# One-input affine steps of a mixer: from VectorE to ScalarE, or folded into their neighbours

## The chip, the core and the metric

The kernel runs on one core of one Trainium2 chip. The metric is the device time of one execution in microseconds (us), the median of several runs. The core's engines are TensorE (PE, with PEld for its weight loads), VectorE (DVE), ScalarE (ACT), GpSimd (POOL) and SyncE (SP), which here issues the DMAs. Each engine works through its own instructions strictly in the order in which they stand; semaphores hold an instruction back until what it reads is there and what it overwrites has been read.

## What is computed

A decoder trunk of two layers over 256 positions of width 1024, in float32. Each layer is a mixer with three branches, a LayerNorm, a retrieval over 16384 one-neuron experts (PEER), and a second LayerNorm. The change lies in the mixer, in its branches A and B:

```python
p = x @ w_in[l]                                   # one input projection, split among the branches
# A: depthwise causal conv of width 4, gates r and i, a linear recurrence, gelu of a second projection
xc = causal_depthwise_conv(xb, conv_w, conv_b)
r = sigmoid(xc @ wa + ba);  i = sigmoid(xc @ wx + bx)
log_a = -8 * r * softplus(-log_a_param)
h = scan(exp(log_a), sqrt(-expm1(2 * log_a)) * (i * xc));   y_a = h * gelu(gb)
# B: RWKV-7, 8 heads of 64
w = -softplus(-(w0 + tanh(xw) @ w2)) - 0.5;  a = sigmoid(a0 + xa @ a2)
kk = k * k_k;  kk = kk / norm(kk, per head);  k = k * (1 + (a - 1) * k_a)
state = state * exp(-exp(w)) - (state @ kk) x (kk * a) + v x k;  y = state @ r
yn = (y - mean) * rsqrt(var + eps) * gn_g + gn_b
y_b = (yn + bonus) * g
# C: latent attention -> y_c;  then merged = sum of sigmoid(gate_n) * (y_n @ P_n), times w_out, LayerNorm
```

## The kernel before, in words

Channels lie on the 128 partitions and positions along the free axis, so a mixer tensor of 512 channels is a tile of 128 x 4 x 256. Every weight tile of 128x1024 comes by DMA into `raw` and is split into two float32r parts: ACT makes `hi` (L84, a cast) and DVE makes `lo = raw - hi` (L88; POOL does so in part of PEER). A projection (`projecting`, L247 to L249) is then 24 matmuls of 128x256, three for each eighth of the contraction: hi times x-high, hi times x-low, lo times x-high. The two PSUM buffers `mm` take the results, so a projection can only start when the one two places before it has been read.

The mixer (function `mixer`) mixes a long chain with many independent projections. The chain is branch B: `rwkv_prep` (decay, keys, gates; L463 to L593), then `rwkv_scan`, which works in four chunks of 64 positions. Before the chunks it inverts a triangular matrix for each head and half chunk by substitution: 31 steps of a multiply (L613) and an add (L615) on DVE, each of which reads the one before, and then transposes up to the tile `t1u` (L623), which TensorE needs for the next matmuls (L638). After the chunks the result `yt` is normalised per head: a Newton iteration for the inverse square root on 128x16 (L172 to L176), `head_bcast` (a copy that repeats each head's value over 64 columns, `hex`, L310, and four transposes on PE, L313), a multiply (L710), the affine step with gn_g and gn_b (L712), two tensor steps (L713, L714) and the split into `ybh` and `ybl` (tiles k and at), which `branch(1, ...)` multiplies with its weights. Everything else is filler: the generators `latent` (branch C), `rg_prep`, `rg_gate` and `rg_scan` (branch A; conv in L729 and L731, gates from L747, gelu from L789), `gates1` and `branch` for branches 2 and 0. `fill(n)` draws n steps from them at points of the chain.

The order that results on the engines is not the order of the source. The framework that builds the program places the instructions of each engine by a schedule of its own when the program is built; on the chip that order is fixed. So an edit of one line can move the instructions around it.

`rsqrt`, `split` and `stream` are shared helpers, so their lines (L84, L88, L166 to L176) stand for many uses; the tile names tell them apart (`wo` is a weight tile of branch 1 or of the output projection).

## Time and profile before

| | |
|---|---|
| median of 3 runs | 2335.33 us (2332.97 to 2336.89) |
| the profiled execution: its own time | 2339.72 us |
| its span, first to last instruction | 2338.0 us |
| PE busy | 2242.7 us, 96% of the span |
| DVE busy | 1790.2 us, 77% |
| ACT busy | 1088.5 us, 47% |
| POOL busy | 278.4 us, 12% |
| mean granted TensorE clock | 0.979 of full speed |

The mixer of layer 0 fills the span from its start to about 345 us, that of layer 1 from about 1170 to 1515 us; PEER lies between and behind. Matmuls overlap each other and their ends are modelled, so a busy PE is not a PE at its peak, but a gap in its row is real. In the clock column 1.00 is full speed (2.4 GHz) and 0.50 the lower level (1.2 GHz).

### The profile page before, as it was taken

The numbers are of one execution on the slowest core, as the hardware profiler recorded it, in microseconds if no ns is written. First come the engines' busy times: TensorE is split into PE (matmuls) and PEld (weight loads), VectorE is DVE, ScalarE is ACT, GpSimd is POOL, SyncE is SP. The second block draws the span as 40 slices with busy tenths as digits, with TensorE's granted clock in tenths as the row PEclk, the third lists the DMA queues.
The fourth block names the chain that finished last, engine by engine and source line by source line (L and its number), as shares of the span: only waits on it lengthen the run. The fifth ranks groups of instructions, "written<-read, shape, count | busy, mean of one in ns | idle before, by whom it ended". The sixth has DMA issues, their size and how long they took to land. (4 is left out here: it accounts for less than half of the span.)

```text
span 2338.0 us, 39856 instructions
## 1 busy us (share of the span) xinstructions
PE 2242.7 (96%) x15748; PEld 1980.1 (85%) x15748; DVE 1790.2 (77%) x3268; ACT 1088.5 (47%) x1635; POOL 278.4 (12%) x220
## 2 busy tenths in 40 slices
PE   7999989999999999999899999899999999999998
PEld 6888879998888888888787888799988888888886
DVE  6777877966788888755666877789668888887556
ACT  4543534445555544444445534344455555444443
POOL 0010016930000000000000100179300000000000
PEclk9998999999999999999999989999999999999999
DMA  6323344555555555655552234445555555556554
GB/s 212 118 79 113 133 164 146 165 184 185 175 170 172 173 176 170 213 196 190 189 174 91 91 109 134 160 142 170 183 184 177 172 171 172 174 171 214 194 193 136
DMA packets 104925, 381.88 MB, mean 163 GB/s; under 512 B 11649, under 2 KB 12161, under 8 KB 104481
## 3 DMA queue, kind: packets, MB, share of 16 engines
q1 hardware_dynamic: 104736, 379.32, 48.7%
q8 instruction: 124, 2.03, 0.3%
q14 instruction: 65, 0.52, 0.1%
HBM read 374.56 MB, written 4.72 MB: 162 GB/s over the span
## 5 line engine op out<-in xcount | busy, mean ns | idle before, releaser
L84 ACT CAST hi<-raw 128x1024 fp32r<-128x1024 f32 x658 | 690.3, 1050 | 756.2 <-PE acc L262 343.7
L88 DVE TENSOR_TENSOR lo<-raw,hi 128x1024 fp32r<-128x1024 f32 x570 | 696.0, 1222 | 250.0 <-ACT hi L84 242.5
L262 PE MATMUL acc<-hi,a 128*128 128x512 f32 x2000 | 554.6, 392 | 0.9 <-ACT a L166 0.9
L247 PE MATMUL mm<-xt,hi 128*128 128x256 f32 x1760 | 516.3, 294 | 23.7 <-ACT hi L84 11.7
L249 PE MATMUL mm<-xt,lo 128*128 128x256 f32 x1760 | 508.5, 290 | 13.9 <-DVE lo L88 10.5
L248 PE MATMUL mm<-xt,hi 128*128 128x256 f32 x1760 | 507.5, 288 | 0.0
L994 PE MATMUL acc<-xt,hi 128*128 128x512 f32 x1344 | 474.4, 399 | 0.0
L262 PEld LDWEIGHTS acc<-hi,a 128*128 128x128 f32 x2000 | 370.9, 188 | 76.2 <-ACT a L166 1.2
L247 PEld LDWEIGHTS mm<-xt,hi 128*128 128x128 f32 x1760 | 345.3, 196 | 31.0 <-ACT hi L84 11.7
L249 PEld LDWEIGHTS mm<-xt,lo 128*128 128x128 f32 x1760 | 344.3, 196 | 20.1 <-DVE lo L88 12.5
L997 PE MATMUL acc<-xt,lo 128*128 128x256 f32 x1344 | 348.7, 280 | 0.0
L248 PEld LDWEIGHTS mm<-xt,hi 128*128 128x128 f32 x1760 | 345.4, 196 | 2.1 <-issue 0.8
L262 PE MATMUL acc<-lo,a 128*128 128x512 f32 x1000 | 311.4, 391 | 0.0
L994 PEld LDWEIGHTS acc<-xt,hi 128*128 128x128 f32 x1344 | 245.4, 188 | 44.4
L88 POOL TENSOR_TENSOR lo<-raw,hi 128x512 fp32r<-128x512 f32 x176 | 251.5, 1455 | 244.9 <-ACT hi L84 243.2
L997 PEld LDWEIGHTS acc<-xt,lo 128*128 128x128 f32 x1344 | 253.5, 189 | 12.1
L262 PEld LDWEIGHTS acc<-lo,a 128*128 128x128 f32 x1000 | 187.7, 188 | 40.6 <-DVE lo L88 0.2
L1002 ACT COPY H<-acc 128x256 f32<-128x256 f32 x168 | 62.7, 373 | 232.0 <-PE acc L994 232.0
L1003 DVE TENSOR_TENSOR H<-H,acc 128x256 f32<-128x256 f32 x168 | 70.1, 417 | 60.8 <-ACT H L1002 60.8
L167 DVE SCALAR_TENSOR_TENSOR a<-H,a 128x1024 fp32r<-128x1024 f32 x64 | 78.4, 1225 | 44.7 <-ACT a L166 44.7
L166 ACT ACTIVATE a<-H 128x1024 fp32r<-128x1024 f32 x64 | 67.9, 1060 | 77.2 <-PE acc L262 76.9
L1094 DVE SCALAR_TENSOR_TENSOR H<-sm,H 128x512 f32<-128x512 f32 x128 | 87.7, 685 | 19.4 <-PE sm L1091 18.6
(356 smaller groups left out, 2381.4 us busy)
## 6 DMA issues: line engine op xcount, KB each, us to landing
raw<-in_uT_dram SPq DMA_DIRECT2D x256, 512.0 KB, 3.5
raw<-in_vt_dram SPq DMA_DIRECT2D x256, 512.0 KB, 3.8
raw<-in_w_in_dram SPq DMA_DIRECT2D x100, 512.0 KB, 3.5
...
```

Source lines behind the costliest of these rows:

```text
L84: A.copy(hi, raw)
L88: eng.tensor_sub(lo[:, c:c + n], raw[:, c:c + n], hi[:, c:c + n].bitcast(F32))
L166: A.activation(hi, src, AF.Copy, scale=scale)
L167: V.scalar_tensor_tensor(lo, src, scale, hi.bitcast(F32), op0=OP.mult, op1=OP.subtract)
L247: T.matmul(pt, h3[:, k, :], xth[:, k, :], start=(k == 0), stop=False)
L248: T.matmul(pt, h3[:, k, :], xtl[:, k, :], start=False, stop=False)
L249: T.matmul(pt, l3[:, k, :], xth[:, k, :], start=False, stop=(k == 7))
L262: T.matmul(acc[b][hf], m[:, bs], w[:, 512 * hf:512 * hf + 512], start=(k == 0 and j == 0), stop=(k == n - 1 and j == 2))
L994: T.matmul(p, h3[:, k, :], xt[:, k].rearrange("p a t -> p (a t)"), start=(k == 0), stop=(k == 7))
L997: T.matmul(p[:, 0:S], l3[:, k, :], xt[:, k, 0], start=False, stop=False)
L1003: V.tensor_add(h, h, p[:, 0:S])
L1094: V.scalar_tensor_tensor(hv, p.rearrange("p (t e) -> p e t", t=8), 1 / GATE_SCALE, hv, op0=OP.mult, op1=OP.mult)
```

## The change

In each layer's mixer:

- `head_bcast`: the copy to `hex` (L310, six per layer) goes from DVE to ACT.
- `kk = k * k_k` (L463, four per layer) goes from DVE to ACT.
- The decay's `+ w0` (L474, four per layer, DVE) disappears: the four results go from PSUM through four ACT tanh with bias w0/2 instead of one ACT tanh over 128x1024 (L475). `hb` in the setup is four columns wider for that.
- The affine step of `t2` (L495, four), the affine step with gn_g and gn_b (L712, four) and the first tap of the conv (L729, four) go from DVE to ACT.
- `at` (L562, one of 128x1024) disappears: its two constants are taken into the two products that follow (L563 and L565), which become scalar_tensor_tensor.
- `rt * 0.5` (L760) disappears into the constants 4 and -4 of the setup; `1 + 0.044715 * gx^2` (L791) disappears into the scale of the ACT square and the product behind it (L793).

```diff
@@ -125,8 +125,8 @@
 
     omm = const.tile([P, L, 14], F32, tag="omm", name="omm")
     V.tensor_scalar(omm, pr[:, :, PC["mix"]:PC["mix"] + 14], -1.0, 1.0, op0=OP.mult, op1=OP.add)
-    hb = const.tile([P, L, 12], F32, tag="hb", name="hb")
-    for i, n in enumerate(("a0", "bx", "v0")):
+    hb = const.tile([P, L, 16], F32, tag="hb", name="hb")
+    for i, n in enumerate(("a0", "bx", "v0", "w0")):
         V.tensor_scalar(hb[:, :, 4 * i:4 * i + 4], pr[:, :, PC[n]:PC[n] + 4], 0.5, None, op0=OP.mult)
     ka = const.tile([P, L, 8], F32, tag="ka", name="ka")
     V.tensor_scalar(ka[:, :, 0:4], pr[:, :, PC["k_a"]:PC["k_a"] + 4], 0.5, None, op0=OP.mult)
@@ -151,8 +151,8 @@
         V.tensor_mul(acc, acc, w)
         V.tensor_scalar(rl, la, -1.0, 0.0, op0=OP.mult, op1=OP.max)
         V.scalar_tensor_tensor(acc, acc, 2.0, rl, op0=OP.mult, op1=OP.add)
-        V.tensor_scalar(sp[:, :, 0:4], acc, 8.0, None, op0=OP.mult)
-        V.tensor_scalar(sp[:, :, 4:8], acc, -8.0, None, op0=OP.mult)
+        V.tensor_scalar(sp[:, :, 0:4], acc, 4.0, None, op0=OP.mult)
+        V.tensor_scalar(sp[:, :, 4:8], acc, -4.0, None, op0=OP.mult)
 
     dram = ctx.enter_context(tc.tile_pool(name="dram", bufs=1, space=bass.MemoryType.DRAM))
     vsave = dram.tile([P, 4, S], F32, tag="vsave", name="vsave")
@@ -307,7 +307,7 @@
 
         def head_bcast(st, b):
             ex = mp.tile([P, 8, 64], F32, tag="hex", name=nm("hex"), bufs=1)
-            V.tensor_copy(ex, st[:, 8 * b:8 * b + 8].unsqueeze(2).to_broadcast([P, 8, 64]))
+            A.copy(ex, st[:, 8 * b:8 * b + 8].unsqueeze(2).to_broadcast([P, 8, 64]))
             p = psm()
             for i in range(4):
                 T.transpose(p[:, i * P:(i + 1) * P], ex[:, 2 * i:2 * i + 2, :].rearrange("p a t -> p (a t)"), ident)
@@ -460,7 +460,7 @@
             k_, kk, t1 = c4("k"), c4("kk"), c4("t1")
             for i in range(4):
                 shifted(T_K + i, k_[:, i, :])
-                V.tensor_scalar(kk[:, i, :], k_[:, i, :], pcol(l, "k_k", i), None, op0=OP.mult)
+                A.activation(kk[:, i, :], k_[:, i, :], AF.Copy, scale=pcol(l, "k_k", i))
                 A.activation(t1[:, i, :], kk[:, i, :], AF.Square)
             fill(8)
             at = c4("at")
@@ -471,8 +471,7 @@
                 A.activation(at[:, i, :], p, AF.Tanh, bias=hb[:, l, i:i + 1], scale=0.5)
                 p = pacc()[:, :S]
                 T.matmul(p, lw[0:64, i * P:(i + 1) * P], tw[0:64, :], start=True, stop=True)
-                V.tensor_scalar(sg[:, i, :], p, pcol(l, "w0", i), None, op0=OP.add)
-            A.activation(sg, sg, AF.Tanh, scale=0.5)
+                A.activation(sg[:, i, :], p, AF.Tanh, bias=hb[:, l, 12 + i:13 + i], scale=0.5)
             V.tensor_scalar(sg, sg, 0.5, 0.5, op0=OP.mult, op1=OP.add)
             fill(8)
             st = small.tile([P, 16], F32, tag="hst", name=nm("hst"), bufs=2)
@@ -492,7 +491,7 @@
                 fill(4)
             t2 = c4("t2")
             for i in range(4):
-                V.tensor_scalar(t2[:, i, :], at[:, i, :], ka[:, l, i:i + 1], ka[:, l, 4 + i:5 + i], op0=OP.mult, op1=OP.add)
+                A.activation(t2[:, i, :], at[:, i, :], AF.Identity, bias=ka[:, l, 4 + i:5 + i], scale=ka[:, l, i:i + 1])
             V.tensor_mul(k_, k_, t2)
             bon = c4("t2")
             for i in range(4):
@@ -559,10 +558,9 @@
                 V.tensor_mul(AR[:, i, :, 0, :], ch(kk)[:, i], ch(sg)[:, i])
                 V.tensor_mul(AR[:, i, :, 1, :], ch(r_)[:, i], e4[:, i])
                 V.tensor_mul(KB[:, i, :, 0, :], ch(k_)[:, i], ch(cum)[:, i])
-            V.tensor_scalar(at, at, -0.5, -0.5, op0=OP.mult, op1=OP.add)
-            V.tensor_mul(at, at, kk)
-            for i in range(4):
-                V.tensor_mul(KB[:, i, :, 1, :], ch(at)[:, i], ch(cum)[:, i])
+            V.scalar_tensor_tensor(at, at, 1.0, kk, op0=OP.add, op1=OP.mult)
+            for i in range(4):
+                V.scalar_tensor_tensor(KB[:, i, :, 1, :], ch(at)[:, i], -0.5, ch(cum)[:, i], op0=OP.mult, op1=OP.mult)
 
             while fillers and fillers[0] is lat:
                 fill(1)
@@ -709,7 +707,7 @@
             for b in range(2):
                 V.tensor_mul(yt[:, :, b * P:(b + 1) * P], yt[:, :, b * P:(b + 1) * P], head_bcast(rs, b))
             for i in range(4):
-                V.tensor_scalar(yt[:, i, :], yt[:, i, :], pcol(l, "gn_g", i), pcol(l, "gn_b", i), op0=OP.mult, op1=OP.add)
+                A.activation(yt[:, i, :], yt[:, i, :], AF.Identity, bias=pcol(l, "gn_b", i), scale=pcol(l, "gn_g", i))
             V.tensor_add(yt, yt, v_)
             V.tensor_mul(yt, yt, g_)
             ybh, ybl = c4("k", F32R), c4("at", F32R)
@@ -726,7 +724,7 @@
             xv = c4("m2")
             for i in range(4):
                 A.copy(xp[:, i, 3:S + 3], (yield from projecting(w_in[l, T_RX + i])))
-                V.tensor_scalar(xv[:, i, :], xp[:, i, 3:S + 3], pcol(l, "conv_w", i), pcol(l, "conv_b", i), op0=OP.mult, op1=OP.add)
+                A.activation(xv[:, i, :], xp[:, i, 3:S + 3], AF.Identity, bias=pcol(l, "conv_b", i), scale=pcol(l, "conv_w", i))
                 for j in range(1, 4):
                     V.scalar_tensor_tensor(xv[:, i, :], xp[:, i, 3 - j:S + 3 - j], pcol(l, "conv_w", 4 * j + i), xv[:, i, :],
                                            op0=OP.mult, op1=OP.add)
@@ -757,8 +755,6 @@
             yield
             V.scalar_tensor_tensor(rt, rt, 1.0, rm, op0=OP.add, op1=OP.mult)
             yield
-            V.tensor_scalar(rt, rt, 0.5, None, op0=OP.mult)
-            yield
             V.scalar_tensor_tensor(it, it, 1.0, xv, op0=OP.add, op1=OP.mult)
             yield
             al = c4("m1")
@@ -786,11 +782,9 @@
             yield
             yield
             g3 = c4("m0")
-            A.activation(g3, gx, AF.Square)
-            yield
-            V.tensor_scalar(g3, g3, 0.044715, 1.0, op0=OP.mult, op1=OP.add)
-            yield
-            V.tensor_mul(g3, g3, gx)
+            A.activation(g3, gx, AF.Square, scale=math.sqrt(0.044715))
+            yield
+            V.scalar_tensor_tensor(g3, g3, 1.0, gx, op0=OP.add, op1=OP.mult)
             yield
             A.activation(g3, g3, AF.Tanh, scale=math.sqrt(2.0 / math.pi))
             yield
```

With the shorter file, line numbers after the change are up to six lower than before. The order of the instructions moves at the places below (buffer numbers differ slightly between the two programs).

VectorE in layer 0's triangular inverse, before: `tmp` and `ti` are the substitution steps, `lo` the weight splits, `m<-xp` the conv.

```order
L613 TENSOR_TENSOR tmp_1545<-lt_1540,ti_1542 64x112
L729 TENSOR_SCALAR m_1328<-xp_1326,pr 128x256
L615 TENSOR_TENSOR ti_1542<-ti_1542,tmp_1545 64x28x4
L731 SCALAR_TENSOR_TENSOR m_1328<-xp_1326,pr,m_1328 128x256
L613 TENSOR_TENSOR tmp_1545<-lt_1540,ti_1542 64x135
L731 SCALAR_TENSOR_TENSOR m_1328<-xp_1326,pr,m_1328 128x256
L615 TENSOR_TENSOR ti_1542<-ti_1542,tmp_1545 64x27x5
L731 SCALAR_TENSOR_TENSOR m_1328<-xp_1326,pr,m_1328 128x256
L613 TENSOR_TENSOR tmp_1545<-lt_1540,ti_1542 64x156
L88 TENSOR_TENSOR lo_1760<-raw_1756,hi_1758 128x1024
L615 TENSOR_TENSOR ti_1542<-ti_1542,tmp_1545 64x26x6
```

A first tap of the conv (L729) and three further taps (L731) stand between the substitution's steps, and `lo_1760` behind them. The same piece with the change:

```order
L611 TENSOR_TENSOR tmp_1544<-lt_1539,ti_1541 64x112
L88 TENSOR_TENSOR lo_1759<-raw_1755,hi_1757 128x1024
L613 TENSOR_TENSOR ti_1541<-ti_1541,tmp_1544 64x28x4
L729 SCALAR_TENSOR_TENSOR m_1327<-xp_1325,pr,m_1327 128x256
L611 TENSOR_TENSOR tmp_1544<-lt_1539,ti_1541 64x135
L729 SCALAR_TENSOR_TENSOR m_1327<-xp_1325,pr,m_1327 128x256
L613 TENSOR_TENSOR ti_1541<-ti_1541,tmp_1544 64x27x5
L729 SCALAR_TENSOR_TENSOR m_1327<-xp_1325,pr,m_1327 128x256
L611 TENSOR_TENSOR tmp_1544<-lt_1539,ti_1541 64x156
L88 TENSOR_TENSOR lo_1791<-raw_1787,hi_1789 128x1024
L613 TENSOR_TENSOR ti_1541<-ti_1541,tmp_1544 64x26x6
```

The conv's first tap is gone from this engine, and the split that stood behind three more conv steps and a substitution multiply (`lo_1760`, now `lo_1759`) stands right behind the first multiply; the next split has moved up into its place.

VectorE at the end of layer 0's recurrence, before, from the second `yt` multiply to the split of `yt` (tile at):

```order
L710 TENSOR_TENSOR yt_2365<-yt_2365,sm_2917 128x4x128
L842 TENSOR_TENSOR mg_1980<-mg_1980,gt_2854 128x256
L712 TENSOR_SCALAR yt_2365<-yt_2365,pr 128x256 x4
L842 TENSOR_TENSOR mg_1980<-mg_1980,gt_2939 128x256
L713 TENSOR_TENSOR yt_2365<-yt_2365,v_687 128x1024
L88 TENSOR_TENSOR wo_3069<-raw_3070,wo_3069 128x1024
L714 TENSOR_TENSOR yt_2365<-yt_2365,g_961 128x1024
L88 TENSOR_TENSOR lo_3088<-raw_3084,hi_3086 128x1024
L88 TENSOR_TENSOR wo_3112<-raw_3113,wo_3112 128x1024
L167 SCALAR_TENSOR_TENSOR at_2930<-yt_2365,k_2929 128x1024
```

All steps of the `yt` chain stand close together, with three weight splits among them. The same piece with the change, from the first `yt` multiply on:

```order
L708 TENSOR_TENSOR yt_2364<-yt_2364,sm_2906 128x4x128
L835 SCALAR_TENSOR_TENSOR gt_2936<-gt_2936,acc_2990 128x256
L88 TENSOR_TENSOR lo_3085<-raw_3081,hi_3083 128x1024
L708 TENSOR_TENSOR yt_2364<-yt_2364,sm_2914 128x4x128
L836 TENSOR_TENSOR mg_1979<-mg_1979,gt_2936 128x256
L88 TENSOR_TENSOR wo_3109<-raw_3110,wo_3109 128x1024
L88 TENSOR_TENSOR lo_3127<-raw_3123,hi_3125 128x1024
L711 TENSOR_TENSOR yt_2364<-yt_2364,v_687 128x1024
L712 TENSOR_TENSOR yt_2364<-yt_2364,g_961 128x1024
L835 SCALAR_TENSOR_TENSOR gt_3005<-gt_3005,acc_3087 128x256
L88 TENSOR_TENSOR lo_3160<-raw_3156,hi_3158 128x1024
L167 SCALAR_TENSOR_TENSOR at_2927<-yt_2364,k_2926 128x1024
```

The four affine steps are gone, and the weight split that stood behind the affine steps and both tensor steps (`lo_3088`, now `lo_3085`) stands ahead of the second `yt` multiply; the following one (`lo_3127`) is ahead of the sum with `v` too.

ScalarE at the same place, before:

```order
L84 CAST hi_3049<-raw_3047 128x1024
L318 ACTIVATE gt_2939<-mm_2946 128x256
L84 CAST wo_3069<-raw_3070 128x1024
L84 CAST wo_3112<-raw_3113 128x1024
L84 CAST hi_3086<-raw_3084 128x1024
L84 CAST hi_3128<-raw_3126 128x1024
L318 ACTIVATE gt_3008<-mm_3015 128x256
L318 ACTIVATE gt_3046<-mm_3053 128x256
L166 ACTIVATE k_2929<-yt_2365 128x1024
```

Casts and gate activations alone stand ahead of the split of `yt` (tile k). The same piece with the change:

```order
L84 CAST hi_3046<-raw_3044 128x1024
L310 COPY hex_2904<-hrs_2830 128x512
L84 CAST hi_3083<-raw_3081 128x1024
L310 COPY hex_2912<-hrs_2830 128x512
L84 CAST wo_3109<-raw_3110 128x1024
L84 CAST hi_3125<-raw_3123 128x1024
L710 ACTIVATE yt_2364<-yt_2364,pr 128x256 x4
L318 ACTIVATE gt_3005<-mm_3012 128x256
L318 ACTIVATE gt_3043<-mm_3050 128x256
```

The two `hex` copies now stand between the casts of weight tiles, and the four affine steps ahead of two gate activations (`gt`), whose PSUM buffers the next projections need.

## Rows read from the trace of the kernel before

**Rows 1.** The page, part 1: busy us, share of the span, instructions.

```profile
PE 2242.7 (96%) x15748; PEld 1980.1 (85%) x15748; DVE 1790.2 (77%) x3268; ACT 1088.5 (47%) x1635; POOL 278.4 (12%) x220
```

**Rows 2.** Stretches, both mixers: length; busy PE, PEld, DVE, ACT, POOL; clock, DMA, GB/s.

```profile
30.00:330.00 300.00, 279.76 (x2266) 256.84 (x2265) 232.26 (x424) 136.62 (x247) 13.72 (x16) 0.95 0.38 127
1185.00:1500.00 315.00, 293.54 (x2320) 266.23 (x2319) 240.16 (x437) 142.82 (x256) 15.32 (x16) 0.95 0.37 122
```

**Rows 3.** Timeline of PE, inverse: start, us, instruction, idle before it and releaser.

```profile
158.65 0.39 PE L249 MATMUL mm<-xt,lo 128*128 128x256 f32 x1 [1.72 <-DVE lo L88]
163.77 0.38 PE L249 MATMUL mm<-xt,lo 128*128 128x256 f32 x1 [1.99 <-DVE lo L88]
...
202.41 1.05 PE L638 MATMUL sm<-t1u,GM 32*32 32x32 f32 x16 [3.90 <-DVE t1u L623]
...
1366.87 1.03 PE L638 MATMUL sm<-t1u,GM 32*32 32x32 f32 x16 [5.13 <-DVE t1u L623]
```

**Rows 4.** Stretches of the inverse, layer 0, and the one behind it; columns as in rows 2.

```profile
176.00:192.00 16.00, 16.00 (x136) 16.00 (x135) 15.04 (x30) 7.54 (x11) 0.00 (x0) 1.00 0.52 167
...
202.00:216.00 14.00, 13.59 (x95) 11.43 (x96) 7.20 (x16) 1.52 (x2) 0.00 (x0) 0.51 0.22 76
```

**Rows 5.** Timeline of DVE inside the inverses: a tap in layer 0, hex in layer 1.

```profile
154.06 0.41 DVE L729 TENSOR_SCALAR m<-xp,pr 128x256 f32<-128x256 f32 x1
...
1322.18 0.42 DVE L310 COPY hex<-bst 128x512 f32<-128x512 f32 x1
...
1323.62 0.69 DVE L593 TENSOR_TENSOR v<-v,sm 128x512 f32<-128x512 f32 x1
```

**Rows 6.** Timeline of PE at the end of the recurrences, both layers.

```profile
292.38 0.39 PE L837 MATMUL acc<-m,lo 128*128 128x256 f32 x1 [0.82 <-DVE lo L88]
297.31 0.39 PE L249 MATMUL mm<-xt,lo 128*128 128x256 f32 x1 [1.95 <-DVE lo L88]
...
307.02 0.28 PE L835 MATMUL acc<-k,wo 128*128 128x256 f32 x1
...
1463.76 0.38 PE L249 MATMUL mm<-xt,lo 128*128 128x256 f32 x1 [2.09 <-DVE lo L88]
```

**Rows 7.** Stretches there, layer 0, then layer 1; columns as in rows 2.

```profile
288.00:298.00 10.00, 7.23 (x57) 6.75 (x57) 9.90 (x12) 4.72 (x6) 0.00 (x0) 0.99 0.49 157
298.00:301.00 3.00, 3.00 (x16) 3.00 (x15) 2.75 (x3) 1.05 (x1) 0.00 (x0) 0.50 0.83 242
...
1465.00:1468.00 3.00, 3.00 (x17) 3.00 (x17) 2.12 (x2) 0.98 (x3) 0.00 (x0) 0.54 0.78 279
```

**Rows 8.** Timeline of DVE there, layer 0.

```profile
281.67 0.43 DVE L310 COPY hex<-hrs 128x512 f32<-128x512 f32 x1
...
286.08 1.38 DVE L712 TENSOR_SCALAR yt<-yt,pr 128x256 f32<-128x256 f32 x4
...
293.38 1.21 DVE L167 SCALAR_TENSOR_TENSOR at<-yt,k 128x1024 fp32r<-128x1024 f32 x1
```

**Rows 9.** Groups of DVE and ACT, 0 to 350 us: busy us, mean ns, idle before.

```profile
L731 DVE SCALAR_TENSOR_TENSOR m<-xp,pr,m 128x256 f32<-128x256 f32 x12 | 5.8, 482 | 0.3
...
L565 DVE TENSOR_TENSOR KB<-at,t 128x256 f32<-128x256 f32 x4 | 1.5, 421 | 0.1
...
L767 ACT ACTIVATE m<-m,sp 128x256 f32<-128x256 f32 x4 | 2.0, 498 | 0.6 <-DVE m L760 0.6
L464 ACT ACTIVATE t<-kk 128x256 f32<-128x256 f32 x4 | 1.7, 413 | 1.4 <-DVE kk L463 1.4
L407 ACT COPY pT<-acc 128x512 f32<-128x512 f32 x2 | 1.2, 592 | 0.0
```

**Rows 10.** Timeline of PE in layer 1, ahead of the inverse and in the chunks.

```profile
1219.87 0.39 PE L247 MATMUL mm<-xt,hi 128*128 128x256 f32 x1 [1.81 <-DVE r L289]
...
1423.47 0.33 PE L662 MATMUL sm<-s,AR 128*64 128x64 f32 x2 [1.48 <-DVE s L684]
```

## The prediction

> **What bounds the kernel now.** I began with the busy times of the engines. TensorE is busy for 96% of the span and VectorE for 77% [rows 1], so whatever VectorE is spared counts only where TensorE stands still for it. The change lies in the mixers alone, so I cut those out next. Between 30 and 330 us (layer 0) TensorE is busy 279.8 of 300 us, between 1185 and 1500 us (layer 1) 293.5 of 315 [rows 2]. That leaves 20.2 and 21.5 us of gaps, 41.7 us together, and no relief of VectorE can bring more than these and what the clock loses through them.
>
> The third look was at the timeline of TensorE: what ended each gap. Two kinds matter.
>
> The first is the triangular inverse of branch B. In it VectorE is busy 15.04 of 16 us [rows 4], the rest being the seams between its short steps. At its end TensorE has run out of filler and waits 3.90 us for `t1u` in layer 0 and 5.13 us in layer 1 [rows 3]. So VectorE sets the moment at which TensorE goes on, and any step taken off VectorE inside the inverse moves that moment by its own length. The waits for `lo` inside it (1.72 and 1.99 us in layer 0 [rows 3]) are no gain of their own: TensorE would only arrive earlier at the wait for `t1u`.
>
> The second is the end of the recurrence, where the normalising of `yt` runs. VectorE is busy 9.90 of 10 us there and TensorE 7.23 [rows 7]; TensorE waits for `lo` twice, 0.82 and 1.95 us in layer 0, and layer 1 shows the second of the pair with 2.09 us [rows 6]. Right behind these gaps the clock stands at 0.50 for 3 us in layer 0 and at 0.54 in layer 1 [rows 7].
>
> **The change part by part.** The sum is made against the profiled execution, span 2338.0 us, own time 2339.72 us. The median of the runs is 2335.33 us, 4.4 us less, and I subtract the same gain from it.
>
> *What VectorE is spared.* Per layer: six `hex` at 0.43 us [rows 8] make 2.6; twelve steps over 128x256 (`t2`, `yt`, conv) at 0.41 [rows 5] make 4.9; eight more of that size (`kk`, `w0`) at about the same 3.3. The 128x1024 steps of `at`, `rt` and `gx` have no row here; four steps over 256 take 1.38 us [rows 8], which I take as their upper end, and half of it as the value: 2.1 for three. Against this, the four products L565 become three-operand steps: 0.482 instead of 0.421 us, 0.25 together [rows 9]. The balance is about 12.6 us per layer, 5% of VectorE's 232 us in layer 0 [rows 2]. Little of it lies on the path.
>
> *Inverse.* Inside it stand three first taps in layer 0 at 0.41 us, 1.23 together, and in layer 1 one `hex` (0.42) and one of the two multiplies of v by it (0.69), which now stands ahead of the inverse: 1.11 [rows 5]. Both count in full, because the wait for `t1u` is longer than that: **-2.3 us**. Ends: -1.5 if the seams grow, -2.6.
>
> *End of the recurrence.* Two `hex` and the four `yt` steps leave VectorE: 0.43 + 0.43 + 1.38 = 2.2 us [rows 8]. Besides, the order moves the `lo` for which TensorE waits ahead of most of the `yt` chain. The gap to be had is 0.82 + 1.95 = 2.8 us [rows 6], in layer 1 about the same. I take 2.4 us, between what is removed and what is there, in each layer: **-4.8 us**. Ends: 0 and -5.6. What is late next is the `yt` chain itself. Its last step ends at 294.6 us [rows 8] and TensorE wants it at 307.0 [rows 6]; 12.4 us of cover take the four or five by which the chain grows (two more hops to ScalarE, the splits moved ahead of it, longer steps).
>
> *Clock.* Before the drop behind these gaps TensorE had stood still for 2.8 of 10 us. With nearly no gap the drop may not come. It lasts about 3 us at half speed, so it costs about 1.5 us in each layer [rows 7]. I take one of the two, **-1.5 us**; ends 0 and -3.
>
> *Ahead of the inverse.* TensorE waits there for VectorE's readings of PSUM, the longest 1.81 us for `r` in layer 1 [rows 10]. Steps of `kk`, `w0`, `t2` and `hex` go out of VectorE's queue in this stretch. I take **-1.0 us**, about half of that one wait; ends 0 and -4.
>
> *What ScalarE gets.* Six `hex` at 0.592 us (a copy of the same size [rows 9]); `kk` at 0.498 (one operand per partition [rows 9]); four tanh at 0.498 each in place of one over 128x1024. Twelve steps carry two operands per partition, and no row has that: at least 0.498, and hardly more than the 0.592 of twice the elements; I take 0.54, nearer to the row with one operand. Together 3.6 + 2.0 + 1 + 6.5 = 13 us per layer, on an engine that is busy 136.6 of 300 us [rows 2]. The cover is its idle half; without it casts come later and VectorE's `lo` with them.
>
> The Trainium skill (ScalarE: Activation LUTs, section What ACT_TABLE_LOAD costs) counts 186 ns plus 0.833 ns per element, and about 93 ns for each operand read per partition. That makes 0.585 us, an estimate, for the steps with two; by it ScalarE would get 0.5 us more per layer and the sum would be the same, since these steps lie beside other work. With one operand the Trainium skill's 0.492 agrees with 0.498, and with none its 0.399 stands against 0.413 [rows 9].
>
> *What gets worse.* In layer 1's chunks the order puts a product over 128x1024 ahead of the state's multiply instead of behind it; TensorE waits 1.48 us there now [rows 10], and I add 0.7. The hops to ScalarE get 0.8. Together **+1.5 us**; ends 0 and +6.
>
> The sum is -2.3 - 4.8 - 1.5 - 1.0 + 1.5 = **-8.1 us**: span 2329.9 us, and 2335.33 - 8.1 = **2327.2 us** for the median. The steps on `rt` and `gx` cost and bring nothing in this sum: they shorten a chain that ends as filler.
>
> **The rivals.**
>
> *Nothing that can be measured.* Only the inverse counts, and the gaps at the end of the recurrence go to some other late instruction, since the whole order is made anew. For it: VectorE's total falls by only 5% there and TensorE is 93% busy. Against it: the moved `lo` stand far ahead of where they stood. -2.3 - 1.0 + 1.5 gives 2333.5 us.
>
> *Slower: the casts get stuck behind `hex`.* ScalarE works strictly in order. The `hex` copy now waits on it for the last Newton step of VectorE, and the next cast stands right behind. Before, that step ended at 281.67 us [rows 8]; with three splits put between the links of the iteration it comes up to 3.7 us later. The wait decides from the point at which the cast behind comes too late for its `lo`: TensorE wants that one at 291.6 us (292.38 less 0.82 [rows 6]), and a cast and a split take some 2.3 us, so from a `hex` later than about 288 us on. If `hex` came 4 us beyond that at the ends of both layers, and the two pairs in the preparations cost 2 us each, TensorE would lose 12 us and about 4 to clock drops behind them: 2335.3 + 16 - 8.1 = 2343 us. Against it: some 3 us of air at the place where I can work it out. The Trainium skill speaks for this rival (ScalarE: Activation LUTs, Rules for kernel authors: multiply and add belong on VectorE, not on ScalarE); the rows agree that a step gets longer by it, 0.41 on VectorE [rows 5] against 0.498 [rows 9], but that decides only where ScalarE is waited for.
>
> *More than forecast.* All gaps at the end of the recurrence go, both clock drops with them, and most of the waits ahead of the inverse: -2.6 - 5.6 - 3 - 4 = -15.2 us, 2320 us. For it: VectorE is the releaser of most gaps. Against it: TensorE would find the next late thing.
>
> **How the numbers follow.** A difference of 0.2%, 4.7 us, is about what a measurement of this kernel can tell from no change; faster then means below 2330.7 us. The forecast (2322 to 2330.7) gets 0.55, more than forecast 0.15, nothing measurable 0.22, slower 0.08. Of the third I count 0.01 as faster and 0.01 as slower. That makes faster 0.71, same 0.20, slower 0.09. The range goes from 2318 to 2336 us: below lies a third of the second case, above it most of the slower one and a little of the third.
>
> **What would show it.** In the profile after: TensorE's wait for `t1u` in layer 0 ending by about 201 us; the waits of TensorE for `lo` between 285 and 300 us gone; no stretch at half clock behind them; VectorE's busy time down by about 25 us, ScalarE's up by about 26; the last step of `yt` still over 5 us ahead of TensorE's first use. The prediction is wrong if TensorE's gaps in the mixers do not shrink by some 8 us, if waits for `hi` or `hex` appear in their place, or if a half-clock stretch comes where none was.

## The result, and the profile after

The changed kernel takes **2319.7 us** (median of 5 runs, 2317.98 to 2327.32), the kernel before in runs alternating with it on the same chip 2336.89 us. The ratio is 0.9935, 95% interval 0.9919 to 0.9952: 15.2 us faster (11.2 to 18.9). A second measurement (further below) gave 0.9943 (0.9928 to 0.9958), 13.3 us. The forecast was 8.1 us; the time lies at the value of the rival "more than forecast". The profiled execution took 2317.98 us, its span is 2316.3 us, the mean granted clock 0.984.

The page after, part 1, beside [rows 1]:

```profile
PE 2232.5 (96%) x15748; PEld 1971.3 (85%) x15748; DVE 1767.0 (76%) x3211; ACT 1110.7 (48%) x1685; POOL 277.9 (12%) x220
```

VectorE lost 23.2 us and ScalarE got 22.2, near what was expected (25 and 26). TensorE's busy time fell by 10.2 us with the same 15748 matmuls: its work is the same, and its mean clock is 0.984 instead of 0.979.

To see where the gaps went, the mixers are cut at the same landmark in both kernels: the first matmul that reads `t1u`. Four stretches: layer 0 from 30 us up to it and from it to the LayerNorm, then the same of layer 1 (columns as in rows 2). Before:

```profile
30.00:202.41 172.41, 158.38 (x1193) 145.78 (x1191) 137.09 (x275) 83.59 (x174) 8.73 (x13) 0.98 0.34 113
202.41:342.73 140.32, 134.11 (x1131) 121.33 (x1131) 102.85 (x169) 54.51 (x75) 5.34 (x4) 0.93 0.41 136
1170.67:1366.87 196.20, 181.02 (x1335) 164.48 (x1336) 149.12 (x289) 95.83 (x193) 11.28 (x15) 0.97 0.37 121
1366.87:1509.20 142.33, 136.04 (x1125) 122.87 (x1125) 102.90 (x169) 54.63 (x75) 5.48 (x4) 0.91 0.41 134
```

After:

```profile
30.00:200.76 170.76, 156.99 (x1184) 143.59 (x1183) 130.02 (x255) 91.08 (x190) 8.81 (x13) 0.98 0.35 113
200.76:334.15 133.39, 132.04 (x1136) 120.09 (x1136) 99.03 (x161) 57.13 (x81) 5.55 (x4) 0.95 0.44 143
1162.58:1355.64 193.06, 179.79 (x1337) 163.78 (x1337) 140.28 (x268) 104.05 (x212) 10.36 (x15) 0.98 0.37 123
1355.64:1487.30 131.66, 129.60 (x1124) 116.98 (x1124) 99.41 (x161) 57.10 (x81) 5.49 (x4) 0.95 0.44 145
```

Length less busy PE is TensorE's idle time: 14.0, 6.2, 15.2 and 6.3 us before, 13.8, 1.4, 13.3 and 2.1 after. Up to `t1u` 2.2 us of gaps went in both layers together, behind it 9.1 us, 11.3 in all. Most of it came from the stretch with the recurrence. The busy time in it fell too, by 2.1 and 6.4 us, and the clock column rose (0.93 to 0.95, 0.91 to 0.95).

The timeline of PE after, at the places of [rows 3, 6, 10]:

```profile
200.76 0.37 PE L636 MATMUL sm<-t1u,GM 32*32 32x32 f32 x3 [4.76 <-DVE t1u L621]
257.62 0.27 PE L660 MATMUL sm<-s,AR 128*64 128x64 f32 x1 [0.57 <-DVE s L682]
298.50 0.28 PE L829 MATMUL acc<-k,wo 128*128 128x256 f32 x1
...
1211.01 0.33 PE L313 MATMUL sm<-ident,hex 128*128 128x128 f32 x1 [1.34 <-ACT hex L310]
...
1355.64 0.25 PE L636 MATMUL sm<-t1u,GM 32*32 32x32 f32 x1 [4.92 <-DVE t1u L621]
...
1410.92 0.27 PE L660 MATMUL sm<-s,AR 128*64 128x64 f32 x1 [1.34 <-DVE s L682]
```

The wait for `t1u` is the largest one left in the mixers. The waits for `lo` at the end of the recurrences have no row any more, in either layer. The wait for the state, 1.48 us in both layers before, shrank to 0.57 and 1.34 us. A new one stands ahead of layer 1's inverse: TensorE waits 1.34 us for a `hex` of ScalarE, where it waited 1.81 us for `r` before.

The timeline of DVE after, end of layer 0's recurrence (some rows), beside [rows 8]:

```profile
282.33 1.22 DVE L88 TENSOR_TENSOR lo<-raw,hi 128x1024 fp32r<-128x1024 f32 x1
283.46 0.68 DVE L708 TENSOR_TENSOR yt<-yt,sm 128x512 f32<-128x512 f32 x1
...
285.53 1.22 DVE L88 TENSOR_TENSOR lo<-raw,hi 128x1024 fp32r<-128x1024 f32 x1
287.33 1.23 DVE L711 TENSOR_TENSOR yt<-yt,v 128x1024 f32<-128x1024 f32 x1 [0.58 <-ACT yt L710]
...
291.20 1.22 DVE L167 SCALAR_TENSOR_TENSOR at<-yt,k 128x1024 fp32r<-128x1024 f32 x1
```

Two splits now end at 283.6 and 286.8 us, ahead of the long steps of `yt`, and VectorE waits 0.58 us for ScalarE's affine steps. The chain ends at 292.4 us, 6.1 us ahead of its first use at 298.50.

Groups of ACT and DVE after, 0 to 350 us, for the prices taken from [rows 9]:

```profile
L310 ACT COPY hex<-hrs 128x512 f32<-128x512 f32 x4 | 2.5, 622 | 2.6 <-DVE hrs L176 2.6
L494 ACT ACTIVATE t<-at,ka 128x256 f32<-128x256 f32 x4 | 2.2, 644 | 0.0
L710 ACT ACTIVATE yt<-yt,pr 128x256 f32<-128x256 f32 x4 | 2.1, 590 | 0.0
...
L563 DVE SCALAR_TENSOR_TENSOR KB<-at,t 128x256 f32<-128x256 f32 x4 | 1.4, 419 | 0.0
```

A ScalarE step with two operands per partition takes 0.59 to 0.64 us, not 0.54. By the Trainium skill (ScalarE: Activation LUTs, What ACT_TABLE_LOAD costs) the estimate had been 0.585. The rows of `yt` (0.590) agree, those of `t2` (0.644) lie a tenth above it. The product with a third operand on VectorE costs nothing more: 0.419 against 0.421.

**The clock.** Layer 1's chunks before, the stretch up to the wait of 1.48 us for the state and the one behind it (columns as in rows 2):

```profile
1410.00:1424.00 14.00, 11.86 (x142) 10.89 (x142) 10.89 (x16) 6.41 (x7) 0.00 (x0) 1.00 0.36 116
1424.00:1434.00 10.00, 9.73 (x66) 8.97 (x64) 7.00 (x8) 1.16 (x2) 0.00 (x0) 0.51 0.60 200
```

The same place after:

```profile
1400.00:1414.00 14.00, 12.66 (x157) 11.69 (x155) 11.31 (x14) 4.82 (x6) 0.00 (x0) 1.00 0.48 156
1414.00:1424.00 10.00, 10.00 (x106) 9.52 (x106) 8.37 (x12) 2.99 (x4) 0.00 (x0) 1.00 0.59 201
```

Before, TensorE had stood still for 2.1 of 14 us and then ran at half clock for 10 us; after, for 1.3 of 14, and it keeps full clock. Ten microseconds at half clock cost some 5 us. But that length belongs to this one execution as much as to the wait: the same wait of 1.48 us in layer 1 is followed by only 3.4 us at half clock in the profiles of e1, e3, e5, e11 and e12 (further below) and by 6.8 us in that of e4; in layer 0 it is followed by 3.4 us (before, e5) or by none (e1, e3, e4, e11, e12). So the two profiles overstate the gain by the clock. All runs for which a clock is listed give a steadier number: span times mean granted clock is what the span would be at full clock, the rest is lost to the clock. This is an estimate, which takes the whole span as bound by TensorE.

| kernel | runs | mean us | at full clock | lost to the clock |
|---|---|---|---|---|
| before | 78 | 2334.1 | 2288.9 | 43.5 |
| the change (both measurements) | 11 | 2320.6 | 2279.2 | 39.6 |
| tail alone | 6 | 2322.8 | 2285.5 | 35.6 |
| tail's `hex` alone | 7 | 2327.1 | 2287.9 | 37.5 |
| tail's affine steps alone | 6 | 2325.3 | 2283.7 | 39.9 |
| all but the tail | 12 | 2328.2 | 2282.2 | 44.2 |
| gate scan's merges alone | 12 | 2326.8 | 2286.2 | 38.9 |
| tail and merges | 6 | 2318.8 | 2281.9 | 35.1 |

(The 1.7 us between span and own time are in neither column.) Of 13.5 us in the means, 9.6 are work and waits, 3.9 the clock. The split is coarse: the clock is listed to three places, one step of which is 2.3 us of a run, and where TensorE would have waited anyway, half clock costs nothing (e10 shows such a place). With the tail alone 5.7 us of waits went, and the full-clock column falls by 3.4. The profiled execution of before, 2339.72 us, lies near the upper end of those 78 runs (2330.2 to 2339.94), which is why the two spans differ by 21.7 us and the medians by less.

### The profile page after: what moved, and what is told of

The parts are those of the page before. It is cut to its first block, busy times and chain, and to the rows that moved or that the text cites. A ratio compares the mean times of both kernels' runs of the same rounds, so it can differ in the third digit from the quotient of the medians.

```text
span 2316.3 us, 39849 instructions
## 1 busy us (share of the span) xinstructions
PE 2232.5 (96%) x15748; PEld 1971.3 (85%) x15748; DVE 1767.0 (76%) x3211; ACT 1110.7 (48%) x1685; POOL 277.9 (12%) x220
```

## The experiments

Differences in us are (ratio less 1) times the median of the kernel before in the same measurement.

### The change in two halves

**e1, the tail alone.** The kernel before with the two `hex` of the tail and the four affine steps of `yt` on ScalarE:

```diff
-def head_bcast(st, b):
+def head_bcast(st, b, act=False):
...
-V.tensor_copy(ex, st[:, 8 * b:8 * b + 8].unsqueeze(2).to_broadcast([P, 8, 64]))
+(A.copy if act else V.tensor_copy)(ex, st[:, 8 * b:8 * b + 8].unsqueeze(2).to_broadcast([P, 8, 64]))
...
-V.tensor_mul(yt[:, :, b * P:(b + 1) * P], yt[:, :, b * P:(b + 1) * P], head_bcast(rs, b))
+V.tensor_mul(yt[:, :, b * P:(b + 1) * P], yt[:, :, b * P:(b + 1) * P], head_bcast(rs, b, True))
...
-V.tensor_scalar(yt[:, i, :], yt[:, i, :], pcol(l, "gn_g", i), pcol(l, "gn_b", i), op0=OP.mult, op1=OP.add)
+A.activation(yt[:, i, :], yt[:, i, :], AF.Identity, bias=pcol(l, "gn_b", i), scale=pcol(l, "gn_g", i))
```

> The kernel before, with only the two hex copies and the four gn steps at the end of the recurrence on ScalarE (2.2 us off VectorE per layer). Theory 1 (TensorE waits for late splits there, and the clock falls behind the gaps): the waits of 0.82 and 1.95 to 2.09 us go in both layers and so do the two short half-clock stretches behind them, 5.7 + 3 = about 9 us less than before. Theory 2 (what helped is the new order of the whole mixer, whichever edit causes it): anything from -10 to +5 us, and gaps that move elsewhere. Theory 3 (VectorE's total time is what counts): 2.2 of 12.6 us per layer, so about 3 us less.

Measured: 2323.2 us against 2333.66, ratio 0.9949 (0.9934 to 0.9965), -11.9 us. In its profile the waits for `lo` at the end of both recurrences are gone.

**e2, all but the tail.** The changed kernel with these steps put back on VectorE (the diff of e1 the other way round).

> The changed kernel with only the end of the recurrence undone: its two hex copies and four gn steps are back on VectorE. Theory 1: the waits for the splits between 285 and 300 us and their half-clock stretches are back, about 9 us slower than the changed kernel, 6 to 8 us faster than before. Theory 2: the parts do not add up with the run of the tail alone. Theory 3: about 14 us faster than before.

Measured: 2328.78 us, ratio 0.9976 (0.9965 to 0.9987), -5.6 us. In layer 1 the two waits for `lo` are back, 0.94 and 2.09 us. In layer 0 only 0.31 us of them is left, and the clock is the likely reason (windows behind the wait for `t1u`):

```profile
199.00:216.00 17.00, 14.87 (x109) 12.79 (x110) 9.38 (x19) 1.04 (x1) 0.00 (x0) 0.50 0.20 62
216.00:233.00 17.00, 17.00 (x114) 14.64 (x114) 6.05 (x12) 2.66 (x4) 0.00 (x0) 0.50 0.31 94
```

Here TensorE stayed at half clock for 34 us, and VectorE, busy for only 6.05 of the last 17 of them, could get ahead of it. The halves give 11.9 + 5.6 = 17.5 us where the whole gives 15.2 and 13.3: they add up within their intervals, so they give no sign that it is the new order as a whole that makes the gain.

### The other half in three parts

**e3, the inverse alone.** The kernel before with the first taps of the conv and the `hex` of v on ScalarE:

```diff
...
-V.tensor_scalar(xv[:, i, :], xp[:, i, 3:S + 3], pcol(l, "conv_w", i), pcol(l, "conv_b", i), op0=OP.mult, op1=OP.add)
+A.activation(xv[:, i, :], xp[:, i, 3:S + 3], AF.Identity, bias=pcol(l, "conv_b", i), scale=pcol(l, "conv_w", i))
...
-V.tensor_mul(v_[:, :, b * P:(b + 1) * P], v_[:, :, b * P:(b + 1) * P], head_bcast(bst, b))
+V.tensor_mul(v_[:, :, b * P:(b + 1) * P], v_[:, :, b * P:(b + 1) * P], head_bcast(bst, b, True))
```

> The kernel before, with only the conv's first taps and the two hex copies of bst on ScalarE. Theory 1: TensorE goes on behind t1u 1.2 us earlier in each layer, 2 to 3 us less in all, and the waits at the end of the recurrence stay as before. Theory 2: anything from -10 to +5 us. Theory 3: 2.5 of 12.6 us per layer, 3 us less.

Measured: 2335.06 us, ratio 1.0006 (0.9992 to 1.002). The mechanism is there: from the first substitution step to TensorE's first matmul behind `t1u` it takes 53.13 us in layer 0 (147.55 to 200.68) and 43.46 in layer 1 (1316.80 to 1360.26), before 54.70 (147.71 to 202.41) and 44.24 (1322.63 to 1366.87), together 2.35 us less. In the changed kernel it is 53.14 and 43.45 us. But the time does not show it. At full clock its runs are 1.6 us shorter than those of before, and they lose 2.8 us more to the clock: four of the twelve stand at 2328.2 to 2329.6 us with a clock of 0.983, five at 2338.9 to 2341.6 us with 0.978.

**e5, the preparation alone.** `kk`, `w0`, `t2` and the `hex` of kk on ScalarE, `at` merged, as in the diff of the change.

> The kernel before with only the steps of the preparation changed: kk, w0 and t2 on ScalarE, at merged, the two hex of kk on ScalarE. Theory 1 (the parts add up; the change without the tail gave -5.6 us, the inverse alone about nothing): the preparation or the gate scan carries the rest. Then TensorE's wait of 1.81 us for r in layer 1 is gone, the inverse begins earlier by 1 to 2 us in each layer, and the time is 3 to 5 us below the kernel before. Theory 2 (the steps lie beside other work, what the change without the tail gave was the clock of its runs): the wait for r stays within 1 us, and the time is within 1.5 us of before. In both the waits for lo at the end of the recurrence stay (0.8 and 2.1 us).

Measured: 2332.59 us, ratio 0.9996 (0.9987 to 1.0005): nothing. TensorE's wait of 1.81 us for `r` is gone and a wait of 1.34 us for ScalarE's `hex` is in its place (1218.06 us). A wait has changed its releaser and stayed.

**e6, the merges of the gate scan alone.** The factor 0.5 of `rt` and the affine step of the gelu, two steps over 128x1024 of VectorE per layer (the setup's constants 8 and -8 become 4 and -4):

```diff
-V.tensor_scalar(rt, rt, 0.5, None, op0=OP.mult)
...
-A.activation(g3, gx, AF.Square)
-V.tensor_scalar(g3, g3, 0.044715, 1.0, op0=OP.mult, op1=OP.add)
-V.tensor_mul(g3, g3, gx)
+A.activation(g3, gx, AF.Square, scale=math.sqrt(0.044715))
+V.scalar_tensor_tensor(g3, g3, 1.0, gx, op0=OP.add, op1=OP.mult)
```

> The kernel before with only the two merged steps of branch A's gate scan and gelu (rt times 0.5, the affine step of the gelu), two steps over 128x1024 less on VectorE per layer. Theory 1 (as I took it ahead of the run: a filler's chain gets shorter, nothing waits for it): within 1.5 us of before. Theory 2 (in layer 1's chunks these steps stand between the recurrence's own steps on VectorE, and so the state's multiply comes earlier): TensorE's wait of 1.48 us for the state in layer 1 shrinks by over 1 us, the stretch of 10.2 us at half clock behind it goes, and the time falls by 3 to 7 us.

Measured: 2327.24 us against 2333.47, ratio 0.9969 (0.9961 to 0.9978), **-7.2 us**, for steps to which I had given nothing. Its windows behind `t1u`, layers 0 and 1:

```profile
201.36:337.39 136.03, 130.75 (x1131) 118.44 (x1131) 101.23 (x167) 54.28 (x75) 5.22 (x4) 0.95 0.44 140
...
1361.82:1498.69 136.87, 131.58 (x1125) 118.89 (x1125) 101.55 (x167) 54.17 (x75) 5.53 (x4) 0.94 0.42 139
```

Idle time went from 6.2 and 6.3 to 5.3 us in each layer, 1.9 us in all; the clock rose from 0.93 and 0.91 to 0.95 and 0.94. Over all runs 2.7 us are work and waits and 4.6 us the clock. How a filler's step reaches TensorE is seen in VectorE's order in layer 1's second and third chunk. Before:

```profile
1406.52 1.87 DVE L793 TENSOR_TENSOR m<-m,m 128x1024 f32<-128x1024 f32 x1
...
1409.56 0.69 DVE L683 TENSOR_TENSOR s<-sm,s 128x512 f32<-128x512 f32 x1
...
1419.95 0.69 DVE L683 TENSOR_TENSOR s<-sm,s 128x512 f32<-128x512 f32 x1 [0.93 <-PE sm L675]
1420.56 2.28 DVE L784 TENSOR_TENSOR_SCAN m<-m,m 128x1024 f32<-128x1024 f32 x1
1422.75 0.67 DVE L684 TENSOR_TENSOR s<-s,pcm 128x512 f32<-128x512 f32 x1
```

With the merges:

```profile
1398.12 1.23 DVE L789 SCALAR_TENSOR_TENSOR m<-m,m 128x1024 f32<-128x1024 f32 x1
1400.21 0.69 DVE L670 COPY VS<-sm 64x512 f32<-64x512 f32 x1 [0.87 <-PE sm L668]
...
1402.85 0.69 DVE L683 TENSOR_TENSOR s<-sm,s 128x512 f32<-128x512 f32 x1
...
1412.51 2.28 DVE L782 TENSOR_TENSOR_SCAN m<-m,m 128x1024 f32<-128x1024 f32 x1
1414.71 0.67 DVE L683 TENSOR_TENSOR s<-sm,s 128x512 f32<-128x512 f32 x1
1415.30 1.22 DVE L795 TENSOR_TENSOR m<-m,m 128x1024 f32<-128x1024 f32 x1
1416.43 0.68 DVE L684 TENSOR_TENSOR s<-s,pcm 128x512 f32<-128x512 f32 x1
```

The filler's chain is two steps shorter. In the second chunk the gelu's product (L793, now L789) stood between the copy `VS` and the state's first step (L683); now it is done ahead of `VS`, where VectorE waits for TensorE anyway. Counted from TensorE's first matmul behind `t1u`, this first step starts at 41.0 us instead of 42.7, and TensorE leaves its wait for the state in the third chunk (L662) at 55.3 us instead of 56.6; in layer 0 this is 55.9 instead of 57.4. In the third chunk the scan (2.28 us) now stands ahead of the state's two steps instead of between them, but a product of 1.22 us has taken its place there, so the wait for the state falls only from 1.48 to 1.34 us in both layers, not by over 1 us as theory 2 had it. Two small waits of 0.33 us (state, for L660) and 0.34 us (a gate) in each layer go with it, and the long stretch at half clock is gone; how much of that is due to the edit, one profile cannot tell, as e1, e3 and e5 have only 3.4 us of it with the wait unchanged. Theory 1 falls, theory 2 holds in its time and its clock, not in the size of its wait.

### What in the tail gives the gain: length or order

**e7, load back on VectorE.** The changed kernel with eight steps behind the affine steps:

```diff
+            for j in range(8):
+                V.tensor_scalar(yt[:, j % 4, :], yt[:, j % 4, :], 1.0, None, op0=OP.mult)
```

> The changed kernel with eight steps over 128x256 put back on VectorE behind the affine steps of yt, multiplying by 1 (8 x 0.345 us, as the four affine steps had it: 2.8 us per layer). Where they stand the rest of VectorE's order is nearly the same. Theory 1 (VectorE sets when TensorE goes on at the end of the recurrence): the waits for lo come back with 1.5 to 2.8 us in each layer, a stretch of 3.4 us at half clock stands behind them, and the time rises by 4 to 9 us above the changed kernel, to 2324 to 2329 us. Rival (the gaps went because the new order put the splits ahead, and VectorE now has air there): no wait over 0.7 us, the time within 2 us of the changed kernel's 2319.7.

Measured: 2322.35 us, ratio to the kernel before 0.9955 (0.9943 to 0.9967), some 2.7 us above the changed kernel's 2319.7 (another measurement, so this difference alone says little; at full clock its runs are 1.1 us longer than the changed kernel's). The load was smaller than I had reckoned (timeline of DVE, then the only wait of PE there in layer 0):

```profile
287.28 1.77 DVE L712 TENSOR_SCALAR yt<-yt 128x256 f32<-128x256 f32 x8
```

```profile
297.99 0.39 PE L833 MATMUL acc<-m,lo 128*128 128x256 f32 x1 [0.38 <-DVE lo L88]
```

1.77 us put back bring a wait of 0.38 us (0.42 in layer 1). VectorE has some 1.4 us of air there now, so the saved length alone was not what decided.

**e11 and e12, the tail's halves.** The kernel before with the two `hex` alone (0.86 us off VectorE per layer), and with the four affine steps alone (1.38 us):

> The kernel before with only the two hex copies of the tail on ScalarE (0.43 us each, 0.86 us per layer off VectorE). In VectorE's order the two splits for which TensorE waits then stand ahead of the last yt product and ahead of the split of yt. Theory 'length' (the gain is the time that leaves VectorE): of the waits for lo, 0.82 and 1.95 us, 0.86 us goes, and the gain is about 2 us for both layers and little of the clock. Theory 'order' (the gain is that splits come ahead of steps of the yt chain): the first split comes some 2.1 us earlier (0.86 and a product of 1.22), the second some 3.3 (0.86, two steps of 1.22), both waits go as in the whole tail, and the gain is 7 to 12 us, as the whole tail's 11.9.

> The kernel before with only the four affine steps of yt on ScalarE (1.38 us per layer off VectorE). The splits then stand ahead of both yt products and ahead of the split of yt. Theory 'length': 1.38 us of the 2.8 us of waits goes in each layer, the second wait for lo stays with about 1.4 us, the gain is about 3 us and the drop of the clock behind it stays. Theory 'order': the first split comes 3.8 us earlier (1.38 and two products of 1.22), the second 2.6 us or more; both waits go, and the gain is 7 to 12 us.

Measured: `hex` alone 2326.76 us against 2335.56, ratio 0.9966 (0.9954 to 0.9979), -7.9 us; affine steps alone 2324.05 us, 0.9959 (0.9945 to 0.9974), -9.6 us. Together they give 11.9 (e1), not 17.5: either one moves the same splits ahead. With the affine steps alone no wait for `lo` is left at the end of either recurrence, so 1.38 us of work took away 2.8 us of waits. With `hex` alone two short ones remain in each layer, 0.36 and 1.01 us in layer 1, in layer 0 (timeline of PE):

```profile
293.61 0.38 PE L249 MATMUL mm<-xt,lo 128*128 128x256 f32 x1 [0.39 <-DVE lo L88]
297.56 0.39 PE L835 MATMUL acc<-m,hi 128*128 128x256 f32 x1 [1.05 <-ACT hi L84]
```

The first is what is left of 0.82 and 1.95 us, though only 0.86 us was taken. The second is new, and its cast had waited for a weight from memory (timeline of ACT):

```profile
296.46 1.04 ACT L84 CAST hi<-raw 128x1024 fp32r<-128x1024 f32 x1 [1.52 <-DMA raw<-in_w_br_dram]
```

That transfer was issued at 292.12 us, when the DMA queue had waited 2.2 us for a step of VectorE, so VectorE still sets when the weight comes. So the affine steps alone decide for "order": 1.38 us taken, 2.8 us of waits gone, 5.2 us less at full clock. `hex` alone is less clear. Of the waits for `lo` 2.4 us went, where "length" had 0.86, but with the new wait for `hi` the net is 1.3 us in layer 0 and 1.5 in layer 1, and of its gain the full-clock column gives only 1.0 us to work and waits and 6.0 to the clock.

**e8, load on ScalarE.** The changed kernel with eight copies on ScalarE at the same place, the test of the rival in which something gets stuck behind ScalarE:

```diff
+            for j in range(8):
+                A.activation(yt[:, j % 4, :], yt[:, j % 4, :], AF.Copy)
```

> The changed kernel with eight copies over 128x256 more on ScalarE at the same place (8 x 0.41 us, 3.3 us per layer). Theory 1 (ScalarE has the air; the chain of yt is 6.1 us ahead of its first use): no new wait of TensorE over 0.7 us, the time within 2 us of the changed kernel's 2319.7. Rival (the casts get stuck behind the affine steps, the case I had called slower): the casts behind come 3.3 us later and their lo with them, TensorE waits 1.5 us or more per layer for lo or for k, and the time rises by 3 to 8 us.

Measured: 2325.07 us, ratio 0.9964 (0.9952 to 0.9975), 5.4 us above the changed kernel. Layer 1, timeline of PE:

```profile
1448.13 0.39 PE L249 MATMUL mm<-xt,lo 128*128 128x256 f32 x1 [1.92 <-DVE lo L88]
```

Timeline of DVE ahead of it:

```profile
1442.97 1.23 DVE L713 TENSOR_TENSOR yt<-yt,v 128x1024 f32<-128x1024 f32 x1 [1.37 <-ACT yt L712]
...
1446.86 1.22 DVE L88 TENSOR_TENSOR lo<-raw,hi 128x1024 fp32r<-128x1024 f32 x1
```

2.55 us more on ScalarE hold the product up on VectorE by 1.37 us, and the split behind it in VectorE's queue comes too late. The rival's mechanism is real here, by way of VectorE's queue: with this load the change has less than 2.55 us of air on ScalarE in layer 1. Part of the lateness is the order, which the added steps changed too: this split stands behind both products of `yt` here, and in the changed kernel between them (1440.16 us, the products at 1439.02 and 1441.30). In layer 0 there is no such wait, but in this run TensorE was at half clock for 27 us behind `t1u` there, so that layer tells nothing.

### VectorE relieved in another way

**e4, four weight splits per layer on GpSimd.** The kernel before with the splits of branch 1's weights there:

```diff
-wb.append(stream(w_br[l, 1, n], V, pair=pair(*slots[n])))
+wb.append(stream(w_br[l, 1, n], G, pair=pair(*slots[n])))
```

> The kernel before, with none of the change's edits; the four weight splits of branch 1 that stand among the yt chain go from VectorE to GpSimd, 4.9 us off VectorE per layer at the end of the recurrence. Theory 1: TensorE's waits for the splits there go as in the change, with their half-clock stretches, 6 to 9 us less than before. Theory 2: no systematic gain, -3 to +5 us. Against both, if GpSimd (two steps of 1.45 us per tile) is late for branch 1: waits for wo in place of those for lo, and no gain.

Measured: 2334.41 us, ratio 1.0001 (0.999 to 1.0011). It takes 4.9 us off VectorE's list in each layer, twice as much as the tail's steps, and gains nothing. Timelines of DVE, at the end of layer 0's recurrence:

```profile
281.72 2.30 DVE L88 TENSOR_TENSOR lo<-raw,hi 128x1024 fp32r<-128x1024 f32 x1
...
284.88 3.40 DVE L712 TENSOR_SCALAR yt<-yt,pr 128x256 f32<-128x256 f32 x4
```

of POOL, and of PE:

```profile
281.46 6.33 POOL L88 TENSOR_TENSOR wo<-raw,wo 128x512 fp32r<-128x512 f32 x4 [4.91 <-ACT wo L84]
```

```profile
292.73 0.39 PE L837 MATMUL acc<-m,lo 128*128 128x256 f32 x1 [2.63 <-DVE lo L88]
```

While GpSimd works, VectorE's split takes 2.30 us instead of 1.22 and the four affine steps 3.40 instead of 1.38 [rows 8]; TensorE waits 2.63 us. Besides, the order is the old one: the `lo` for which TensorE waits is still split behind both long products of `yt` (from 291.46 us on). How much of the 4.9 us either of the two ate is not shown. The Trainium skill (Perfetto Trace Analysis, Optimizing Scalar/DVE Operations) says that work of a saturated VectorE may go to ScalarE or even to GpSimd, and that GpSimd might not help, as the two share a read port to SBUF. The stretched steps agree with that; that the port is the reason, no run here shows.

### The two parts that count, and the change once more

**e9, tail and merges.** The kernel before with the edits of e1 and e6.

> The kernel before with the two parts that gained by themselves: the tail (two hex and the four affine steps of yt on ScalarE, -11.9 us alone) and the merges of the gate scan (-7.2 us alone). Preparation and inverse are left as before. Theory 1 (these two carry the whole change; preparation and inverse bring nothing): the time is that of the changed kernel within 3 us, some 2317 to 2323 us, less than the two alone give together (-19.1) because both take away the same stretches at half clock in layer 1's chunks. Rival (the new order of the whole, with preparation and inverse in it, is what counts): the gain stays with the larger of the two, 2321 to 2326 us, and waits for lo or for the state come back.

Measured: 2318.91 us against 2333.49, ratio 0.9935 (0.9922 to 0.9949). That is the whole change's gain in time with a part of its edits. It is not the same by its parts: at full clock its runs are 2.7 us longer than the changed kernel's, near what the inverse saves on its path (2.35 us), and they lose 4.5 us less to the clock. Why the clock takes that back is open. Idle time behind `t1u` is 2.3 and 2.2 us:

```profile
201.59:333.52 131.93, 129.65 (x1131) 117.74 (x1131) 99.39 (x161) 56.82 (x81) 5.42 (x4) 0.96 0.44 144
...
1354.96:1486.35 131.39, 129.18 (x1125) 116.86 (x1125) 99.31 (x161) 56.89 (x81) 5.44 (x4) 0.96 0.44 145
```

**e10, the changed kernel again.**

> The changed kernel unaltered, a second time, beside the run with the two parts. Expected: 2318 to 2323 us, again 0.992 to 0.996 of the kernel before. If the lengths at half clock vary from run to run with nothing in the instructions to explain it, the waits of TensorE in this second profile are the same within 0.1 us, and the stretches behind the wait for t1u differ between the two profiles (13.7 us in both layers in the first); if the waits decide it alone, the stretches are the same too.

Measured: 2319.74 us, ratio 0.9943 (0.9928 to 0.9958). Between the two profiles of one program the stretches behind `t1u` are the same, but an earlier wait is not (timeline of PE, first profile, then second):

```profile
71.45 0.39 PE L247 MATMUL mm<-xt,hi 128*128 128x256 f32 x1 [0.69 <-DVE v L289]
```

```profile
71.87 0.39 PE L247 MATMUL mm<-xt,hi 128*128 128x256 f32 x1 [2.17 <-DVE v L289]
```

In the first TensorE was at half clock from 65 to 68.4 us, in the second at full clock there; counted from the wait before it, it came to this one 1.5 us earlier and waited 1.5 us longer. That half-clock stretch, ahead of a wait for VectorE, cost nothing. So my expectation had both halves wrong: the waits differ and the stretches behind `t1u` do not.

## Why the prediction came out as it did

The direction was right and the size about half: 8.1 us forecast, 15.2 and 13.3 measured. The time missed the forecast's own 2322 to 2330.7 us and came out in the rival to which the prediction gave 0.15; it lies 1.7 us above the lower end of the whole range. The waits named for the inverse and the tail were the right ones. What was missing is the gate scan and most of the clock.

**Inverse (-2.3): right on the path, not seen in the time.** From the first substitution step to TensorE's first matmul behind `t1u` the change saves 1.56 and 0.79 us, 2.35 together (e3), and `t1u` in layer 0 ends its wait at 200.76 us, as "by about 201" said. That it would count in full in the time is what e3 does not show (1.0006): its runs lose as much more to the clock.

**Ahead of the inverse (-1.0): not seen.** In gaps of TensorE up to `t1u` this term and the inverse brought 2.2 us instead of 3.3, e5 shows no gain in time, and e9 leaves both out and is no slower. The wait for `r` was exchanged for one for `hex`: the hops to ScalarE on the way to a transpose, which I had priced at 0.8 us, stand in exactly that place.

**End of the recurrence (-4.8): right in effect, 5.7 us of waits went** (0.82 + 1.95 + 0.82 + 2.09), at the upper end of its bounds. But the working was in part the wrong one: "I take 2.4 us, between what is removed and what is there" reckons with the 2.2 us that leave VectorE. e12 and e7 show that the place of the splits in the queue counts for more: 1.38 us removed take away all the waits for `lo`, and 1.77 us put back bring back 0.4 us per layer. (e11's 0.86 us remove most of them, but bring a wait for `hi`.)

**What gets worse (+1.5), and "the steps on rt and gx cost and bring nothing": the step that failed.** Behind `t1u` 9.1 us of gaps went; less the tail's 5.7 that leaves 3.4 us gained in the chunks and in small gaps, where I had put 0.7 us lost. I read from the order that a product of 128x1024 stands ahead of the state's multiply and took that as a new delay. It does stand there (1.22 us), but where the scan of 2.28 us had stood, and the wait for the state fell by 0.14 us in layer 1. What I had put at nothing, two steps fewer in the filler, moved a product from in front of the state's step in the second chunk, and TensorE leaves its wait in the third 1.3 to 1.5 us earlier in each layer (e6). A filler whose result nobody waits for still stands in VectorE's queue in front of steps that TensorE does wait for. e6: 7.2 us.

**Clock (-1.5): mis-sized, 3.9 us** in the means over all runs. I looked at the two drops behind the waits for `lo` alone and took one of them. The larger one, some 10 us at half clock in layer 1's chunks, stood behind a wait of 1.48 us that I had used in the sum without looking at the clock behind it. Neither is a fixed price: that stretch is 3.4 us long in other profiles, and in e3 and e6 no half clock follows the two waits for `lo` in layer 0.

With the terms put right the sum is 2.2 + 5.7 + 3.4 us of gaps and 3.9 us of clock, 15.2 us, beside 15.2 and 13.3 measured. That it fits so well is partly luck: the gaps, 11.3 us, come from one pair of profiles, and the means over the runs give work and waits 9.6 us.

**What would show it.** The five signs came, the busy times roughly: `t1u` by 200.76 us, no waits for `lo` between 285 and 300 us, no half clock behind them (TensorE's clock is 1.00 from 290 to 300 us), busy times by -23.2 and +22.2 us, the last `yt` step 6.1 us ahead (12.4 before, so the chain's cover shrank by more than the four or five reckoned). Two of the signs against it came as well, and small: the wait for `hex`, and a stretch at half clock from 273.3 to 276.7 us where none was; the second profile of the same program has full clock there. ScalarE's price of 0.54 us was too low by 0.05 to 0.10 us, which changed nothing in the sum, as its cover stood.

**The rivals.** "Nothing measurable" falls: the gaps did not go to the next late instruction, except at `r`. "More than forecast" came nearest in time; its terms for the tail, the clock and the path of the inverse (5.6, 3 and 2.6 us) were near, that for the stretch ahead of the inverse (4 us) was not, and the chunks were missing from it, so its time was met with some luck. "Slower" did not happen: the two `hex` of layer 0's tail start at 279.70 and 281.47 us, well ahead of the 288 us from which they would have hurt, ScalarE stands idle for the last Newton step by 0.63 us in layer 0 and 0.17 in layer 1, and no late cast holds TensorE up. But e8 shows that there is not much air: 2.55 us more on ScalarE, with the order that came with them, bring a wait of 1.92 us in layer 1 by way of VectorE's queue.
